# Sample columns of a state-space stage: joined on chip, or stored within the prompt's rows

## The chip, the cores and the metric

The kernel runs on one core of one Trainium2 chip. Its time is the device time of one launch in microseconds (us); lower is better. Three runs of the kernel before took 3122.86, 3125.23 and 3131.07 us; the median is 3125.23 us.

## The reference

One inference step of one decoder layer, in float32, for a prompt of 2048 tokens and for 8 samples of 4 tokens each, with the same weights. The part that the change touches is the S5 group: 512 of the channels of `h @ w_in` form 32 groups of 16, and each group drives a complex diagonal state of 64 entries.

```python
h = rms_norm(x, p['norm_mix'])
z = h @ p['w_in']
u, xin, bg, cg = jnp.split(z, ...)
y_ssm, s_re, s_im = s5_ssm(u, ...)          # s[t] = a * s[t-1] + B u[t];  y = Re(C s) + D u
y_ssm = jax.nn.gelu(y_ssm)
y_ssm = y_ssm * jax.nn.sigmoid(y_ssm @ p['w_glu'] + p['b_glu'])
conv_y, conv_buf = causal_dwconv(cg * xin, p['conv_w'], conv_prev)
y_conv = bg * conv_y
mixed = jnp.concatenate([rms_norm(y_ssm, ...), rms_norm(y_conv, ...)], axis=-1)
x = x + mixed @ p['w_out']
```

The prompt starts from a zero state, the samples from given states. The last states of both (`s_re`, `s_im`) are outputs. Cross-attention and a ConvFFN follow; the change leaves them alone.

## The kernel before

The tokens are cut into five pieces of 416 columns (`NP`); the fifth holds 384 columns of the prompt and the 32 of the samples. Every float32 weight and input is split into a high and a low part, and a product is three matmuls (`mm3`, L367 to L369). The program is one order written out by hand: TensorE (PE) works through the large products, and after each group of matmuls a hook lets the small streams (Python generators) issue a step. A `yield PAUSE` in a stream means "go on at the next hook". Every engine executes its own instructions strictly in the order in which they were issued.

**First stage** (to about 197 us): `u = h @ w_in`, piece by piece. `u_out` (L781) multiplies each tile of `u` by the row norm on GpSimd (POOL, L786) and stores it: the prompt's columns into `u_d`, of 256 columns for each of 8 token offsets, and the samples' 32 columns into a DRAM tensor of their own, `us_d`.

**Conv stage** (about 185 to 672 us): PE computes the short-conv group, 20 conv tiles (four channel tiles by five pieces), each of eight groups of nine matmuls on `mm` banks with a hook behind each: 160 hooks in all. After each conv tile follow `conv_in`, `conv_mid` and `conv_out` on VectorE (DVE), ScalarE (ACT) and POOL. The state-space work rides on the hooks as a stream called `slow`, made of three generators one after another:

- `state_inputs` (L951): 16 rounds of two groups. A round loads `uc` (128 partitions, two groups of 264 columns) from `u_d` (`load_u`, L861), multiplies by `gc` on PE (L994), and copies the result into `st` on ACT (L996, L997). DVE and POOL turn and scan `st` meanwhile. A round takes two or three hooks.
- `scan` (L1142): combines the blocks of the scan, and puts out the samples' last states (`sf`, L1147) by two transposes on PE (L1137).
- `state_outputs` (L1047): 16 rounds of four hooks. `back` (L1062) prepares a block on DVE (L1065, L1067, L1068) and POOL (L1069); `enter` (L1072) builds `scat`, what PE multiplies with, on DVE and POOL (L1081), with the samples' starting states copied in (L1075), and takes the prompt's last state from the block's last column (`sfin`, L1084). PE then makes two pairs of products (L1115 with `uc`, L1116 with `scat`) with a hook between them, and ACT applies GELU (L1117). Round c's `uc` and `scat` have two buffers each.

The samples come into these rounds by copies on POOL. All 32 groups of them are loaded from `us_d` once (L966), and in each round eight columns per group are joined to the tile that the DMA has filled:

```python
G.tensor_copy(out=uc[:, :, 256:264], in_=us_[:, 0, 2 * c:2 * c + 2, :])     # L989, state_inputs
G.tensor_copy(out=uc[:, :, 256:264], in_=us_[:, 1, 2 * c:2 * c + 2, :])     # L1108, state_outputs
G.tensor_copy(out=ysm[:, g2, :], in_=yg[:, :, 256:264])                     # L1123, the way out
```

The results go to `y_d`, the samples' through `ysm` to `ys_d`, and `p3_load` (L1325 on) reads both at the start of the next stage, the fifth piece first.

All DMAs named here go through one queue, SyncE's (SP), in order: the weights (`wraw`, L86), the inputs of the conv stage (`araw`, L176), the loads of the rounds, and the stores (L258), which are collected and issued at the next tick.

Of the kernel before, what the change touches and what calls it, by code (L numbers as in the profile page):

```python
# [208 lines left out]
def tile_hymba_step(ctx: ExitStack, tc: tile.TileContext, I: dict, O: list):  # L209
# [22 lines left out]

    x0_d, x1_d, x2_d = per_piece("x0"), per_piece("x1"), per_piece("x2")
    h3_d, o_d, yc_d = per_piece("h3"), per_piece("oo"), per_piece("yc", 4)
    u_d = dt("u_d", [512, NB, NCH])
    us_d = dt("us_d", [512, NT, 8])
    y_d = dt("y_d", [512, NB, NCH])
    ys_d = dt("ys_d", [512, NT, 8])
    kd_d = dt("kd_d", [256, 512])
    to_d = dt("to_d", [128, 32, 2, 128])  # L240
    g_d = dt("g_d", [128, 32, 128])
# [539 lines left out]
    def u_out(p, us):  # L781
        yield PAUSE
        w, c0 = CW[p], CPP * p
        for j in range(4):
            u = us[j]
            G.tensor_tensor(out=u, in0=u, in1=rs_p[p], op=ALU.mult)  # L786
            store(out=u_d[j * 128:(j + 1) * 128, :, c0:c0 + w], in_=u[:, 0:8 * w].rearrange("p (s c) -> p s c", s=8))
            if p == 4:
                store(out=us_d[j * 128:(j + 1) * 128], in_=u[:, 384:416].rearrange("p (s c) -> p s c", s=NT))
            yield  # L790

    rate[0] = 2
    srate[0] = 1
    slow.add(load_params())
# [64 lines left out]
    us_ = sp_.tile([128, 2, 32, 8], F32, name="us")  # L859

    def load_u(c):  # L861

        uc = py.tile([128, 2, 264], F32, tag="uc", name="uc", bufs=2)
        for i in range(2):
            g = 2 * c + i
            SY.dma_start(out=uc[:, i, 0:NCH], in_=u_d[16 * g:16 * g + 16].rearrange("p s c -> s p c"))
        return uc


# [81 lines left out]
    def state_inputs():  # L951
        ld = {}

        def load(c):
            g2 = slice(2 * c, 2 * c + 2)
            uc = load_u(c)
            gc = py.tile([128, 2, 2, 128], F32, tag="tcn", name="gc", bufs=2)[:, :, 0, :]
            SY.dma_start(out=gc, in_=g_d[:, g2, :])
            ld[c] = (uc, gc)

        G.memset(us_, 0.0)
        tb = phases()
        load(0)
        usv = us_d.rearrange("(g p) j b -> j p g b", p=16)
        for j in range(NT):
            SY.dma_start(out=us_[16 * j:16 * j + 16, 1], in_=usv[j])  # L966
        load(1)
        for _ in range(4):
            yield PAUSE
        V.tensor_copy(out=us_[64:128, 0], in_=us_[0:64, 1])  # L970
        ready, turned, scanned = False, 0, 0

        def recur(upto, n):

# [12 lines left out]
        for c in range(16):
            uc, gc = ld.pop(c)
            G.tensor_copy(out=uc[:, :, 256:264], in_=us_[:, 0, 2 * c:2 * c + 2, :])  # L989
            recur(c, 1)  # L990
            yield PAUSE
            for i in range(2):
                ps = aux()
                PE.matmul(ps[:, 0:264], lhsT=gc[:, i, :], rhs=uc[:, i, :], start=True, stop=True)  # L994
                h = slice(i * 64, (i + 1) * 64)
                S.copy(out=st[h, 0, c, :], in_=ps[0:64, 0:264])  # L996
                S.copy(out=st[h, 1, c, :], in_=ps[64:128, 0:264])  # L997
# [48 lines left out]

    def state_outputs():  # L1047
        yd = y_d.rearrange("(g q) t c -> g t q c", q=16)
        ysd = ys_d.rearrange("(g q) j b -> j q g b", q=16)
        ysm = py.tile([128, 32, 8], F32, name="ysm")  # L1050
        ld = {}

        def load(c):
# [18 lines left out]
        def enter(c):  # L1072

            sc = py.tile([128, 2, 264], F32, tag="scat", name="scat", bufs=2)
            G.tensor_copy(out=sc[:, :, 256:264], in_=s0s[:, 2 * c:2 * c + 2, :])  # L1075
            V.memset(sc[:, :, 0:1], 0.0)
            m1, m2 = parts.pop(c)
            for a in range(2):
                h = slice(a * 64, (a + 1) * 64)
                for r in range(2):  # L1080
                    (G if r else V).tensor_tensor(out=sc[r * 64:(r + 1) * 64, a, 1:256], in0=m1[h, r, 0:255],  # L1081
                                                  in1=m2[h, r, 0:255], op=ALU.add if r else ALU.subtract)
            for r in range(2):
                G.tensor_tensor(out=sfin[:, r, c:c + 1], in0=m1[:, r, 255:256], in1=m2[:, r, 255:256],  # L1084
                                op=ALU.add if r else ALU.subtract)
            ent_[c] = sc

        ent_ = {}
# [13 lines left out]
        for c in range(16):  # L1102
            if c + 1 < 16:
                enter(c + 1)
            if c + 2 < 16:
                back(c + 2)
            uc, tcn, oc = ld.pop(c)
            G.tensor_copy(out=uc[:, :, 256:264], in_=us_[:, 1, 2 * c:2 * c + 2, :])  # L1108
            yield PAUSE
            sc = ent_.pop(c)  # L1110
            g2 = slice(2 * c, 2 * c + 2)
            yg = py.tile([128, 2, 264], F32, tag="yg", name="yg", bufs=2)
            for i in range(2):
                ps = aux()
                PE.matmul(ps[:, 0:264], lhsT=tcn[:, i, :], rhs=uc[:, i, :], start=True, stop=False)  # L1115
                PE.matmul(ps[:, 0:264], lhsT=oc[:, i, :], rhs=sc[:, i, :], start=False, stop=True)  # L1116
                S.activation(out=yg[:, i, :], in_=ps[:, 0:264], func=AF.Gelu_apprx_tanh)  # L1117
                if i == 0:
                    yield PAUSE
            if c + 2 < 16:  # L1120
                load(c + 2)
            yield PAUSE
            G.tensor_copy(out=ysm[:, g2, :], in_=yg[:, :, 256:264])  # L1123
            for i in range(2):
                store(out=yd[2 * c + i], in_=yg[:, i, 0:256])
            yield PAUSE
        for j in range(NT):
# [5 lines left out]
    def state_out(pl, src, n, dsts):  # L1133

        for i in range(2):
# [3 lines left out]
            V.tensor_copy(out=e[0:n], in_=ps[0:n, 0:128])  # L1139
            store(out=dsts[i], in_=e[0:n])  # L1140

    def scan():  # L1142
# [991 lines left out]
```

## Time and profile before

| what | value |
|---|---|
| median of three runs | 3125.23 us |
| the profiled execution, its own time | 3123.47 us |
| its span, first to last instruction | 3121.3 us |
| PE busy | 2899.6 us (93%) |
| DVE busy | 1461.2 us (47%) |
| ACT busy | 1109.9 us (36%) |
| POOL busy | 1180.9 us (38%) |
| mean granted clock of TensorE | 0.969 of full speed |

"Busy" is the time that an engine spent on instructions; what matters here is the rest: time in which PE stands idle, and the instruction that ended that idle time. The clock column (PEclk) is the TensorE clock granted over a stretch, as a share of full speed: 1.0 is 2.4 GHz, and the engine's other level, 1.2 GHz, is 0.5. A stretch with a value between them had both.

### The profile page before, as it was taken

The page shows a single profiled execution, that of the slowest core. Times are in us where ns is not written, and L with a number is a line of the kernel's source. Part 1 is how long each engine was busy: PE and PEld are TensorE (multiplying, and loading weights), DVE is VectorE, ACT ScalarE, POOL GpSimd, SP SyncE. Part 2 cuts the span into 40 slices and gives each one's busy share as a digit, 9 for nine tenths or more (in the row PEclk, how much of TensorE's full clock was granted, in tenths as well). Part 3 has the DMA queues.
Part 4 walks back from the last instruction along what each step waited for, and adds up shares of the span by engine and source line. Part 5 has one row for each costly group of instructions (what it writes and reads, how often), then busy time and mean ns, then how long its engine had stood idle before and what let it go on. Part 6 is the DMA issues. An engine that isn't in the chain of part 4 may idle for free.

```text
span 3121.3 us, 41741 instructions
## 1 busy us (share of the span) xinstructions
PE 2899.6 (93%) x15536; PEld 2794.6 (90%) x15536; DVE 1461.2 (47%) x2698; ACT 1109.9 (36%) x2152; POOL 1180.9 (38%) x1352
## 2 busy tenths in 40 slices
PE   8867857798999999999999999999999999999998
PEld 7767856687999999999999999999999999999997
DVE  5747844445444434345453334345433333355544
ACT  5334322145444444433332232224322222243332
POOL 3654464435334001335343322324223323245554
PEclk9888978899999999999999999999999999999999
DMA  8454432237335112555642121213312112134331
GB/s 231 135 151 119 115 119 89 87 111 219 110 106 162 62 56 66 166 189 197 212 153 61 55 61 54 61 55 117 122 56 61 57 59 62 48 108 138 108 112 55
DMA packets 387337, 335.91 MB, mean 108 GB/s; under 512 B 81121, under 2 KB 361239, under 8 KB 387103
## 3 DMA queue, kind: packets, MB, share of 16 engines
q1 hardware_dynamic: 364079, 299.30, 32.2%
q10 hardware_dynamic: 23056, 33.96, 3.0%
q8 instruction: 122, 2.00, 0.3%
q14 instruction: 80, 0.66, 0.1%
HBM read 259.98 MB, written 75.29 MB: 107 GB/s over the span
## 4 chain that ended last, share of the span: by engine, by line
PE 55%; DVE 2%; DMA 2%; issue 1%; POOL 1%; ACT 1%; SPq 0%; ACTq 0%; DVEq 0%; POOLq 0%
PE g L368 5%; PE g L369 5%; PE g L367 5%; PE u L368 5%; PE d L367 5%; PE u L367 5%; PE u L369 5%; PE d L369 5%; PE d L368 5%; PE mm L368 3%; PE mm L367 3%; PE mm L369 3%; DMA out_dram<-orow 1%; PE aux L368 1%; POOL wlo L98 1%
## 5 line engine op out<-in xcount | busy, mean ns | idle before, releaser
L98 POOL TENSOR_TENSOR wlo<-wraw,whi 128x512 fp32r<-128x512 f32 x489 | 644.0, 1340 | 895.7 <-ACT whi L94 846.9
L367 PE MATMUL mm<-xh,whi 128*128 128x416 f32 x1600 | 596.9, 373 | 3.6 <-ACT whi L94 3.1
L368 PE MATMUL mm<-xl,whi 128*128 128x416 f32 x1600 | 575.2, 360 | 4.5 <-POOL xl L159 4.5
L369 PE MATMUL mm<-xh,wlo 128*128 128x416 f32 x1600 | 572.2, 358 | 3.0 <-POOL wlo L98 2.8
L2023 DVE TENSOR_TENSOR xac<-d,xac 128x416 f32<-128x416 f32 x440 | 258.2, 590 | 252.6 <-PE d L369 250.2
L367 PE MATMUL d<-acth,whi 128*128 128x416 f32 x880 | 311.3, 354 | 18.1 <-DVE xac L2023 16.9
L94 ACT CAST whi<-wraw 128x1024 fp32r<-128x1024 f32 x256 | 266.9, 1045 | 172.0 <-PE d L368 129.8
L367 PEld LDWEIGHTS mm<-xh,whi 128*128 128x128 f32 x1600 | 311.6, 195 | 14.2 <-ACT whi L94 3.8
L368 PEld LDWEIGHTS mm<-xl,whi 128*128 128x128 f32 x1600 | 311.1, 194 | 10.8 <-POOL xl L159 5.9
L369 PEld LDWEIGHTS mm<-xh,wlo 128*128 128x128 f32 x1600 | 310.1, 194 | 7.8 <-POOL wlo L98 4.9
L368 PE MATMUL u<-xl,whi 128*128 128x416 f32 x880 | 312.0, 355 | 1.4 <-POOL xl L159 0.7
L368 PE MATMUL g<-xl,whi 128*128 128x416 f32 x880 | 311.9, 354 | 0.0
L367 PE MATMUL g<-xh,whi 128*128 128x416 f32 x880 | 310.6, 353 | 0.0
L367 PE MATMUL u<-xh,whi 128*128 128x416 f32 x880 | 309.8, 352 | 0.8 <-ACT xh L158 0.6
L369 PE MATMUL g<-xh,wlo 128*128 128x416 f32 x880 | 309.7, 352 | 0.0
L369 PE MATMUL d<-acth,wlo 128*128 128x416 f32 x880 | 309.6, 352 | 0.0
L369 PE MATMUL u<-xh,wlo 128*128 128x416 f32 x880 | 308.5, 351 | 0.0
L368 PE MATMUL d<-actl,whi 128*128 128x416 f32 x880 | 308.0, 350 | 0.2 <-DVE actl L2004 0.2
L1183 DVE SCALAR_TENSOR_TENSOR t<-E,par,t 128x416 f32<-128x416 f32 (+1 forms) x220 | 153.9, 700 | 266.8 <-ACT t L1991 264.2
L159 POOL TENSOR_TENSOR xl<-araw,xh 128x416 fp32r<-128x416 f32 x100 | 115.1, 1153 | 418.0 <-ACT xh L158 386.5
L367 PEld LDWEIGHTS d<-acth,whi 128*128 128x128 f32 x880 | 165.2, 188 | 27.3 <-DVE xac L2023 24.6
L2000 DVE TENSOR_TENSOR t<-t,g 128x416 f32<-128x416 f32 x110 | 64.4, 586 | 260.4 <-PE g L369 260.3
(463 smaller groups left out, 4947.2 us busy)
## 6 DMA issues: line engine op xcount, KB each, us to landing
wraw<-in_w_up_dram SPq DMA_DIRECT2D x66, 512.0 KB
wraw<-in_w_gate_dram SPq DMA_DIRECT2D x66, 512.0 KB
wraw<-in_w_down_dram SPq DMA_DIRECT2D x66, 512.0 KB
araw<-x SPq DMA_DIRECT2D x120, 208.0 KB
xres<-x SPq DMA_DIRECT2D x80, 208.0 KB
x<-xo ACTq DMA_DIRECT2D x80, 208.0 KB
x<-xT ACTq DMA_DIRECT2D x40, 208.0 KB
araw<-oo SPq DMA_DIRECT2D x40, 208.0 KB
```

The source lines that it names most:

```text
L94: self.nc.scalar.copy(out=hi, in_=r)
L98: eng.tensor_tensor(out=lo[:, s], in0=r[:, s], in1=hi[:, s], op=ALU.subtract)
L159: (eng or nc.vector).tensor_tensor(out=lo[:, 0:n], in0=src, in1=hi[:, 0:n], op=ALU.subtract)
L367: PE.matmul(ps, lhsT=wh, rhs=xh, start=start, stop=False)
L368: PE.matmul(ps, lhsT=wh, rhs=xl, start=False, stop=False)
L369: PE.matmul(ps, lhsT=wl, rhs=xh, start=False, stop=stop)
L1183: V.scalar_tensor_tensor(out=out[:, 0:n], in0=E[:, tap * w:tap * w + n], scalar=c, in1=out[:, 0:n], op0=ALU.mult, op1=ALU.add)
L2000: V.tensor_tensor(out=t, in0=t, in1=ps_[:, 0:NP], op=ALU.mult)
L2023: V.tensor_tensor(out=x, in0=ps[:, 0:NP], in1=x, op=ALU.add)
```

## The change

`u_d` gets 272 columns for each token offset and `y_d` 264, so that the samples' columns stand behind the prompt's 256 in the same rows. For the fifth piece `u_out` multiplies into one of two tiles `ends` (zeroed once) by three POOL operations: the prompt's 48 columns, the samples in columns 256 to 264 at token offsets 0 to 3 (what L1108 joined), and the samples again in columns 264 to 272 at offsets 4 to 7 (what L989 joined). One store writes it all. The loads of the rounds bring the joined tile; the copies L989, L1108 and L1123, the tile `us_` with its loads, memset and copy, and `us_d` and `ys_d` go. The products of `state_inputs` have 272 columns, `st` too. The copy of the starting states in `enter` moves from POOL to ACT. The 32 one-column operations on `sfin` become six on DVE at the end of `scan`. The samples' last states are put out at the end of `state_outputs`, and the pauses around the two removed steps go: a round of `state_outputs` now takes three hooks. `p3_load` reads the samples from `y_d`.

```diff
-    u_d = dt("u_d", [512, NB, NCH])
-    us_d = dt("us_d", [512, NT, 8])
-    y_d = dt("y_d", [512, NB, NCH])
-    ys_d = dt("ys_d", [512, NT, 8])
+    u_d = dt("u_d", [512, NB, 272])
+    y_d = dt("y_d", [512, NB, 264])
...
     def u_out(p, us):
...
-            G.tensor_tensor(out=u, in0=u, in1=rs_p[p], op=ALU.mult)
-            store(out=u_d[j * 128:(j + 1) * 128, :, c0:c0 + w], in_=u[:, 0:8 * w].rearrange("p (s c) -> p s c", s=8))
-            if p == 4:
-                store(out=us_d[j * 128:(j + 1) * 128], in_=u[:, 384:416].rearrange("p (s c) -> p s c", s=NT))
+            cols = slice(j * 128, (j + 1) * 128)
+            if p < 4:
+                G.tensor_tensor(out=u, in0=u, in1=rs_p[p], op=ALU.mult)
+                store(out=u_d[cols, :, c0:c0 + w], in_=u[:, 0:8 * w].rearrange("p (s c) -> p s c", s=8))
+            else:
+                e = ends[j % 2]
+                for o, a, n in ((e[:, :, 0:w], 0, 8), (e[:, 0:NT, w:w + 8], 384, NT), (e[:, NT:8, w + 8:w + 16], 384, NT)):
+                    z = slice(a, a + n * (w if a == 0 else 8))
+                    G.tensor_tensor(out=o, in0=u[:, z].rearrange("p (s c) -> p s c", s=n),
+                                    in1=rs_p[p][:, z].rearrange("p (s c) -> p s c", s=n), op=ALU.mult)
+                store(out=u_d[cols, :, c0:c0 + w + 16], in_=e)
...
     def state_inputs():
...
-        G.memset(us_, 0.0)
...
-        for j in range(NT):
-            SY.dma_start(out=us_[16 * j:16 * j + 16, 1], in_=usv[j])
...
-        V.tensor_copy(out=us_[64:128, 0], in_=us_[0:64, 1])
...
-            G.tensor_copy(out=uc[:, :, 256:264], in_=us_[:, 0, 2 * c:2 * c + 2, :])
...
     def state_outputs():
...
-            G.tensor_copy(out=sc[:, :, 256:264], in_=s0s[:, 2 * c:2 * c + 2, :])
+            S.copy(out=sc[:, :, 256:264], in_=s0s[:, 2 * c:2 * c + 2, :])
...
-            for r in range(2):
-                G.tensor_tensor(out=sfin[:, r, c:c + 1], in0=m1[:, r, 255:256], in1=m2[:, r, 255:256],
-                                op=ALU.add if r else ALU.subtract)
...
-            G.tensor_copy(out=uc[:, :, 256:264], in_=us_[:, 1, 2 * c:2 * c + 2, :])
             yield PAUSE
...
             yield PAUSE
-            G.tensor_copy(out=ysm[:, g2, :], in_=yg[:, :, 256:264])
             for i in range(2):
-                store(out=yd[2 * c + i], in_=yg[:, i, 0:256])
-            yield PAUSE
-        for j in range(NT):
-            store(out=ysd[j], in_=ysm[j * 16:(j + 1) * 16])
+                store(out=yd[2 * c + i], in_=yg[:, i, :])
+        yield PAUSE
+        state_out(sp_, sf_.pop().rearrange("p r b g -> p r (b g)"), 128,
...
     def scan():
...
-        yield PAUSE
-        yield PAUSE
-        yield PAUSE
-        state_out(sp_, sf.rearrange("p r b g -> p r (b g)"), 128,
...
+        V.tensor_tensor(out=t, in0=ek[:, :, :, 15], in1=rp[:, :, 15].unsqueeze(1).to_broadcast(SE), op=ALU.mult)
+        V.tensor_tensor(out=t, in0=t, in1=last[:, :, :, 15], op=ALU.add)
...
     def p3_load(p):
...
-                SY.dma_start(out=y[:, 384:416].rearrange("p (s c) -> p s c", s=NT), in_=ys_d[j * 128:(j + 1) * 128])
+                SY.dma_start(out=y[:, 384:416].rearrange("p (s c) -> p s c", s=NT), in_=y_d[j * 128:(j + 1) * 128, 0:NT, 256:264])
```

POOL's order in the middle of `state_outputs`, one conv tile of the kernel before (`scat` is the right side of L1116, `st` the block, `ysm` the samples' results, `y` the conv tile):

```order
L1201 COPY halc<-E 128x2
L1271 TENSOR_TENSOR y<-y,rs_133 128x416
L1123 COPY ysm<-yg 128x16
L159 TENSOR_TENSOR xl<-araw,xh 128x416
L1075 COPY scat<-s0s 128x2x8
L1081 TENSOR_TENSOR scat<-st,mb 64x255 x2
L1084 TENSOR_TENSOR sfin<-st,mb 128x1 x2
L1069 TENSOR_TENSOR st<-st,ph 128x2x256
L1108 COPY uc<-us 128x2x8
```

and the like place with the change:

```order
L1202 COPY halc<-E 128x2
L1272 TENSOR_TENSOR y<-y,rs_131 128x416
L1079 TENSOR_TENSOR scat<-st,mb 64x255 x2
L1067 TENSOR_TENSOR st<-st,ph 128x2x256
L159 TENSOR_TENSOR xl<-araw,xh 128x416 x2
```

Of a round only `scat` and `st` are left on POOL; nothing that PE needs for the product with `uc` is issued there any more.

POOL's order at the end of the first stage, where the fifth piece of `u` goes out and the conv stage's inputs (`xl`) and weights (`wlo`) follow, in the kernel before:

```order
L786 TENSOR_TENSOR u<-u,rs_137 128x416 x4
L159 TENSOR_TENSOR xl<-araw,xh 128x416 x3
L98 TENSOR_TENSOR wlo<-wraw,whi 128x512 x2
L961 MEMSET us 128x512
L98 TENSOR_TENSOR wlo<-wraw,whi 128x512 x2
L159 TENSOR_TENSOR xl<-araw,xh 128x416
L98 TENSOR_TENSOR wlo<-wraw,whi 128x512 x4
L989 COPY uc<-us 128x2x8
```

and with the change:

```order
L792 TENSOR_TENSOR ends_169<-u,rs_135 128x8x48
L792 TENSOR_TENSOR ends_169<-u,rs_135 128x4x8 x2
L792 TENSOR_TENSOR ends_170<-u,rs_135 128x8x48
L792 TENSOR_TENSOR ends_170<-u,rs_135 128x4x8 x2
L792 TENSOR_TENSOR ends_169<-u,rs_135 128x8x48
L792 TENSOR_TENSOR ends_169<-u,rs_135 128x4x8 x2
L792 TENSOR_TENSOR ends_170<-u,rs_135 128x8x48
L792 TENSOR_TENSOR ends_170<-u,rs_135 128x4x8 x2
L159 TENSOR_TENSOR xl<-araw,xh 128x416 x3
L98 TENSOR_TENSOR wlo<-wraw,whi 128x512 x4
L159 TENSOR_TENSOR xl<-araw,xh 128x416
L98 TENSOR_TENSOR wlo<-wraw,whi 128x512 x4
```

Twelve operations into two tiles in turn stand where four stood, ahead of the same `xl`; the first join, behind eight `wlo`, is gone.

SP's order where the rounds of `state_inputs` begin (`gc` is the matrix of L994), before:

```order
L866 DMA uc<-u_d 128x1x256 x2
L958 DMA gc<-g_d 128x2x128
L966 DMA us<-us_d 16x32x8 x4
L866 DMA uc<-u_d 128x1x256 x2
L958 DMA gc<-g_d 128x2x128
```

and with the change:

```order
L872 DMA uc<-u_d 128x1x272 x2
L964 DMA gc<-g_d 128x2x128
L872 DMA uc<-u_d 128x1x272 x2
L964 DMA gc<-g_d 128x2x128
```

The four loads of the samples' columns, of 512 pieces of 32 bytes each, no longer stand between the loads of the first two rounds.

## Rows read from the trace of the kernel before

**Rows 1.** The page's part 2, the span in 40 slices, PE.

```profile
PE   8867857798999999999999999999999999999998
```

**Rows 2.** Busy time by stretch: PE, PEld, DVE, ACT, POOL, then PEclk, DMA share, GB/s.

```profile
215.00:335.00 120.00, 97.00 (x460) 89.41 (x461) 89.57 (x158) 54.10 (x126) 55.55 (x62) 0.92 0.42 122
...
388.00:625.00 237.00, 162.54 (x687) 147.52 (x686) 105.10 (x155) 49.70 (x102) 116.22 (x166) 0.83 0.32 97
632.00:672.00 40.00, 38.58 (x206) 37.04 (x205) 12.34 (x29) 10.67 (x23) 15.48 (x20) 1.00 0.29 85
```

**Rows 3.** Waits of PE, 190 to 640 us: total, times, longest.

```profile
PE aux L1115 <- POOL uc L1108: 74.5, 15, 11.9
PE aux L994 <- POOL uc L989: 23.0, 9, 10.1
PE aux L994 <- POOL dz L903: 17.1, 1, 17.1
PE aux L1137 <- DVE sf L1147: 8.5, 1, 8.5
```

**Rows 4.** Timeline of PE, 384 to 454 us: start, duration, instruction, idle before.

```profile
385.27 0.35 PE L367 MATMUL mm<-xh,whi 128*128 128x416 f32 x1
...
385.84 0.35 PE L367 MATMUL mm<-xh,whi 128*128 128x416 f32 x1
...
400.70 1.25 PE L1115 MATMUL aux<-uc,tcn 128*128 128x264 f32 x2 [11.87 <-POOL uc L1108]
...
452.91 0.61 PE L1115 MATMUL aux<-uc,tcn 128*128 128x264 f32 x2
...
453.60 0.55 PE L367 MATMUL mm<-xh,whi 128*128 128x416 f32 x1
```

**Rows 5.** Timeline of POOL, 388 to 401 us.

```profile
389.16 6.18 POOL L98 TENSOR_TENSOR wlo<-wraw,whi 128x512 fp32r<-128x512 f32 x4
...
397.39 1.49 POOL L1081 TENSOR_TENSOR scat<-st,mb 64x255 f32<-64x255 f32 x2
398.96 0.33 POOL L1084 TENSOR_TENSOR sfin<-st,mb 128x1 f32<-128x1 f32 x2
399.25 1.25 POOL L1069 TENSOR_TENSOR st<-st,ph 128x512 f32<-128x512 f32 x1
400.45 0.19 POOL L1108 COPY uc<-us 128x16 f32<-128x16 f32 x1
```

**Rows 6.** Timeline of DVE, 388 to 520 us.

```profile
392.59 1.63 DVE L1067 TENSOR_TENSOR st<-st,mc 128x512 f32<-128x512 f32 x1
...
444.68 0.41 DVE L1081 TENSOR_TENSOR scat<-st,mb 64x255 f32<-64x255 f32 x1 [9.49 <-issue]
...
445.58 0.70 DVE L1065 TENSOR_TENSOR mc<-ek,rp 128x512 f32<-128x512 f32 x1
...
447.46 1.12 DVE L1068 TENSOR_TENSOR mb<-st,ph 128x512 f32<-128x512 f32 x1
...
510.88 0.59 DVE L1251 TENSOR_TENSOR xi<-mm,rs 128x416 f32<-128x416 f32 x1 [3.39 <-PE mm L369]
...
515.48 0.59 DVE L1270 TENSOR_TENSOR y<-y,mm 128x416 f32<-128x416 f32 x1
```

**Rows 7.** Timelines of POOL, SP and DVE, 182 to 216 us.

```profile
186.23 4.96 POOL L786 TENSOR_TENSOR u<-u,rs 128x416 f32<-128x416 f32 x4 [1.24 <-ACT rs L438]
...
199.81 1.37 SPq L866 DMA_DIRECT2D uc<-u_d  x2
...
201.72 2.05 SPq L966 DMA_DIRECT2D us<-us_d  x4
...
206.34 0.70 DVE L970 COPY us<-us 64x256 f32<-64x256 f32 x1 [6.93 <-DMA uc<-u_d]
```

**Rows 8.** Waits of SP's DMA queue, 0 to 800 us.

```profile
SPq L258 <- POOL y L1271: 62.3, 11, 10.9
```

**Rows 9.** Groups of instructions of DVE by line, 388 to 625 us.

```profile
L162 DVE SCALAR_TENSOR_TENSOR xl<-araw,par,xh 128x416 fp32r<-128x416 f32 x16 | 13.0, 811 | 41.7 <-ACT xh L161 41.7
```

More of the change, by code (lines that the diff above doesn't have):

```diff
@@ L785, in u_out @@
             u = us[j]
-            G.tensor_tensor(out=u, in0=u, in1=rs_p[p], op=ALU.mult)
-            store(out=u_d[j * 128:(j + 1) * 128, :, c0:c0 + w], in_=u[:, 0:8 * w].rearrange("p (s c) -> p s c", s=8))
-            if p == 4:
-                store(out=us_d[j * 128:(j + 1) * 128], in_=u[:, 384:416].rearrange("p (s c) -> p s c", s=NT))
+            cols = slice(j * 128, (j + 1) * 128)
[9 more added lines that the diff above has]
+                store(out=u_d[cols, :, c0:c0 + w + 16], in_=e)
             yield
+    ends = [p1.tile([128, NB, 64], F32, name=f"ends{i}") for i in range(2)]
+    for e in ends:
+        G.memset(e, 0.0)
     rate[0] = 2
@@ L853, in tile_hymba_step @@
     sp_ = ss_.enter_context(pool("states", side="left"))
-    st = sp_.tile([128, 2, 16, 264], F32, name="st")
+    st = sp_.tile([128, 2, 16, 272], F32, name="st")
     s0 = sp_.tile([128, 2, 8, 16], F32, name="s0")
@@ L857, in tile_hymba_step @@
     py = spy.enter_context(pool("py", side="right"))
-    us_ = sp_.tile([128, 2, 32, 8], F32, name="us")
     def load_u(c):
-        uc = py.tile([128, 2, 264], F32, tag="uc", name="uc", bufs=2)
+        uc = py.tile([128, 2, 272], F32, tag="uc", name="uc", bufs=2)
         for i in range(2):
             g = 2 * c + i
-            SY.dma_start(out=uc[:, i, 0:NCH], in_=u_d[16 * g:16 * g + 16].rearrange("p s c -> s p c"))
+            SY.dma_start(out=uc[:, i, :], in_=u_d[16 * g:16 * g + 16].rearrange("p s c -> s p c"))
         return uc
@@ L959, in load @@
             ld[c] = (uc, gc)
-        G.memset(us_, 0.0)
         tb = phases()
         load(0)
-        usv = us_d.rearrange("(g p) j b -> j p g b", p=16)
-        for j in range(NT):
-            SY.dma_start(out=us_[16 * j:16 * j + 16, 1], in_=usv[j])
         load(1)
@@ L993, in state_inputs @@
                 ps = aux()
-                PE.matmul(ps[:, 0:264], lhsT=gc[:, i, :], rhs=uc[:, i, :], start=True, stop=True)
+                PE.matmul(ps[:, 0:272], lhsT=gc[:, i, :], rhs=uc[:, i, :], start=True, stop=True)
                 h = slice(i * 64, (i + 1) * 64)
-                S.copy(out=st[h, 0, c, :], in_=ps[0:64, 0:264])
-                S.copy(out=st[h, 1, c, :], in_=ps[64:128, 0:264])
+                S.copy(out=st[h, 0, c, :], in_=ps[0:64, 0:272])
+                S.copy(out=st[h, 1, c, :], in_=ps[64:128, 0:272])
             if c + 2 < 16:
@@ L1048, in state_outputs @@
         yd = y_d.rearrange("(g q) t c -> g t q c", q=16)
-        ysd = ys_d.rearrange("(g q) j b -> j q g b", q=16)
-        ysm = py.tile([128, 32, 8], F32, name="ysm")
         ld = {}
@@ L1107, in state_outputs @@
             uc, tcn, oc = ld.pop(c)
-            G.tensor_copy(out=uc[:, :, 256:264], in_=us_[:, 1, 2 * c:2 * c + 2, :])
             yield PAUSE
             sc = ent_.pop(c)
-            g2 = slice(2 * c, 2 * c + 2)
             yg = py.tile([128, 2, 264], F32, tag="yg", name="yg", bufs=2)
@@ L1114, in state_outputs @@
                 ps = aux()
-                PE.matmul(ps[:, 0:264], lhsT=tcn[:, i, :], rhs=uc[:, i, :], start=True, stop=False)
+                PE.matmul(ps[:, 0:264], lhsT=tcn[:, i, :], rhs=uc[:, i, 0:264], start=True, stop=False)
                 PE.matmul(ps[:, 0:264], lhsT=oc[:, i, :], rhs=sc[:, i, :], start=False, stop=True)
@@ L1122, in state_outputs @@
             yield PAUSE
-            G.tensor_copy(out=ysm[:, g2, :], in_=yg[:, :, 256:264])
             for i in range(2):
-                store(out=yd[2 * c + i], in_=yg[:, i, 0:256])
-            yield PAUSE
-        for j in range(NT):
-            store(out=ysd[j], in_=ysm[j * 16:(j + 1) * 16])
+                store(out=yd[2 * c + i], in_=yg[:, i, :])
+        yield PAUSE
+        state_out(sp_, sf_.pop().rearrange("p r b g -> p r (b g)"), 128,
+                  [o[0].rearrange("b (g a) n -> (b g) (a n)", a=2) for o in (sre_s, sim_s)])
+        yield PAUSE
         state_out(sp_, sfin, 16, [o[0, 0].rearrange("(g a) n -> g (a n)", a=2) for o in (sre_p, sim_p)])
@@ L1140, in state_out @@
             store(out=dsts[i], in_=e[0:n])
+    sf_ = []
     def scan():
@@ L1146, in scan @@
         cmul(sp_, sf[:, 0], sf[:, 1], s0[:, 0], s0[:, 1], a4[:, 0:1, :].to_broadcast(sh), a4[:, 1:2, :].to_broadcast(sh), sh, "scm")
-        V.tensor_tensor(out=sf, in0=sf, in1=st[:, :, :, 256:264].rearrange("p r g b -> p r b g"), op=ALU.add)
-        yield PAUSE
-        yield PAUSE
-        yield PAUSE
-        state_out(sp_, sf.rearrange("p r b g -> p r (b g)"), 128,
-                  [o[0].rearrange("b (g a) n -> (b g) (a n)", a=2) for o in (sre_s, sim_s)])
+        V.tensor_tensor(out=sf, in0=sf, in1=st[:, :, :, 264:272].rearrange("p r g b -> p r b g"), op=ALU.add)
+        sf_.append(sf)
         yield
@@ L1174, in scan @@
         V.memset(ek[:, :, :, 0:1], 0.0)
+        yield
+        SE = [128, 2, 16]
+        t, m2 = (sp_.tile(SE, F32, tag="sfe", name="sfe", bufs=2) for _ in range(2))
+        V.tensor_tensor(out=t, in0=ek[:, :, :, 15], in1=rp[:, :, 15].unsqueeze(1).to_broadcast(SE), op=ALU.mult)
+        V.tensor_tensor(out=t, in0=t, in1=last[:, :, :, 15], op=ALU.add)
+        V.tensor_tensor(out=m2, in0=t[:, ::-1], in1=ph[:, 1, :, 15].unsqueeze(1).to_broadcast(SE), op=ALU.mult)
+        V.tensor_tensor(out=t, in0=t, in1=ph[:, 0, :, 15].unsqueeze(1).to_broadcast(SE), op=ALU.mult)
+        for r, op in ((0, ALU.subtract), (1, ALU.add)):
+            V.tensor_tensor(out=sfin[:, r], in0=t[:, r], in1=m2[:, r], op=op)
         yield
```

## Prediction

> **What bounds the kernel now.** I read the page's slices first. From slice 11 to 39 PE is busy in at least nine tenths of every slice; only the small step 5 below reaches that far [rows 1]. What can be won lies ahead of that, in the conv stage, so I read busy time by stretch next. From 632 to 672 us, where no round of the state-space work is left, PE is busy 38.6 of 40 us at the full clock (PEclk 1.00, that is 2.4 GHz). From 388 to 625 us, the 16 rounds of `state_outputs`, it is busy 162.5 of 237 us at 0.83, a mixture of 2.4 and 1.2 GHz [rows 2]. The other engines have room there: DVE 105, ACT 50, POOL 116 of 237 us.
>
> The waits of PE say who ends the idle time: 74.5 us until the join of `uc` in `state_outputs` (L1108), 23.0 us until the join in `state_inputs` (L989), once 17.1 us at the first of these rounds, and 8.5 us for the samples' last states (L1137 on `sf`) [rows 3]. The 17.1 us are put down to a memset of `dz` that was issued right behind the first join; the first product needs the join, not the memset.
>
> The timeline shows why a copy of 0.19 us holds PE for 11.9 us [rows 4, 5]. POOL works in order: four splits of weights (6.2 us), two halves of `scat` for the next round (1.5), `sfin`, `st` for the round after (1.25), and only then the copy on which PE waits. The queue ahead of the copy is the cost, not the copy.
>
> **The price of PE's work.** Three matmuls take 0.57 us at full clock, so a hook (nine) takes 1.71 us; a pair of products of L1115 and L1116 takes 0.69 us [rows 4]. The 16 rounds hold 16 x 4 - 3 = 61 hooks and 32 pairs: 61 x 1.71 + 22.1 = 126.4 us. The stretch took 237 us; 74.5 are waits, and the remaining 36 are matmuls at the low clock, which I read as following the stalls.
>
> **The change, part by part.**
>
> 1. *Rounds of `state_outputs`.* With L1108 gone, L1115 needs only loads issued two rounds ahead, and L1116 needs a `scat` that was issued a round ahead. Two pauses become one, so a round has three hooks: 16 x 3 - 2 = 46 hooks and 32 pairs, 100.8 us for PE alone; the 15 hooks set free run behind without rounds, 25.7 us. What is late next is the chain through DVE and POOL. In one round `enter` and `back` hold DVE from 444.68 to 448.58, 3.90 us [rows 6], then `st` on POOL takes 1.25 [rows 5] before the next `enter`: 5.15 us, 82.4 for 16. Each conv tile holds DVE from 510.88 to 516.07, 5.19 us with its wait for ACT [rows 6]; 46 hooks hold 5.75 tiles, 29.8 us. Splitting inputs (`xl`) takes 13.0 us over 61 hooks [rows 9], 9.8 over 46. The four weight splits ahead of the second `scat` add 6.2 [rows 5]. Sum 128.2, more than PE's 100.8, so I take it: 128.2 + 25.7 = 153.9 against 237, **-83 us**. Ends: PE alone gives 126.5 (-110); if half the waits and half the low-clock loss stay, 126.5 + 55 (-55).
>
>    Do DVE and POOL get in each other's way? A DVE operation on 512 elements takes 0.70 us alone and 1.63 beside a weight split [rows 6]; the splits take 1.55 each in that run, and a POOL operation of that size 1.25 alone [rows 5]. So a pair takes 1.63, not 0.70 + 1.25 = 1.95: they hinder each other, but overlap in part. My 3.90 us already holds that hindrance (1.12 us for one of the three). The Trainium skill, page "SBUF — State Buffer", section "Who interferes with whom", is stricter: a VectorE operation with two inputs in SBUF and a GpSimd operation that reads SBUF fully block each other for the whole instruction. By that rule the total would be 3038 us (worked out under the rivals); the 1.63 agrees with it only in part.
>
> 2. *Rounds of `state_inputs`, 215 to 335 us.* Some 44 hooks and 32 single products (half a pair, 0.35 us): 86.4 us of 120. The rest is the 23.0 us of waits and 10.6 of low clock. The join goes, but DVE is busy 89.6 of the 120 us [rows 2], and ACT, which empties the banks of L994 in order, stands behind copies that wait for DVE's scans. I let about half of the waits come back there: 23 + 3 of clock - 12 = **-14 us**; ends 0 and -34.
>
> 3. *The first product (17.1 us).* Without the join it waits for its loads. These now start later: POOL's four operations on `u` took 4.96 us, 1.24 each [rows 7]; each tile gets two small ones more (0.19 as the copy in [rows 5]), and the third tile waits until the first store has landed, about 2.6 us after its issue (the load of the samples ends its issue at 203.77, DVE starts on it at 206.34) [rows 7]. POOL is then free 2.9 us later, and SP, which stands behind the `xl` on POOL, issues the first `uc` at 202.7 instead of 199.8. Two loads of 1.4 us, 0.5 for `gc` (estimated like one of the four in 2.05 us) and 2.6 to land: 207.2 instead of 214.9. **-7 us**; ends +3 (only the delay stays) and -12.
>
> 4. *The samples' last states.* The transposes move to the end of `state_outputs`, where `sf` is long ready: **-8.5 us**; ends 0 (another wait in the same place, since DVE's scan chain there is kept) and -12 with the clock. The six operations that replace `sfin` add 1 to 2 us to DVE ahead of round 0, inside the same slack.
>
> 5. *`p3_load`.* Four loads of 128 pieces become four of 512 pieces of 32 bytes at the start of the next stage. Four such loads were issued in 2.05 us and landed 2.6 us later [rows 7]. **+3 us**; ends 0 and +6.
>
> 6. *Nothing for the rest.* The 64 small POOL operations that go cost PE only through the waits counted above. The 16 copies now on ACT meet an engine that is busy 50 of 237 us [rows 2]; should it be late, L1116 waits. Eight columns more in 32 products are 0.3 us. The two memsets stand at the start, ahead of loads that POOL awaits anyway; if uncovered, about 1 us.
>
> Sum: -83 - 14 - 7 - 8.5 + 3 = -109.5. The profiled execution took 3123.5 us, 1.8 below the median; 3014 for it, **3016 us** for the median.
>
> **The rivals.**
>
> *DVE and POOL strictly in turn.* If each of the three operations of `back` had to wait out a POOL operation (0.70 + 0.75) they would take 4.35 us instead of 3.0: 16 x 1.35 = +22, **3038 us**. For it: 1.63 beside a split. Against it: the pair's 1.95.
>
> *SP's queue takes the place of the join.* At a conv tile's end SP stands up to 10.9 us for POOL's `y` [rows 8], and the loads of a later round stand behind. They need 10.9 + 1.4 + 2.6 = 14.9 us; from the end of a round's products to the use of what is loaded then there are five hooks and two pairs, 9.9. Six tiles x 5.0 = 30, with the low clock (36 per 74.5) 44: **3060 us**. Against it: in the trace these 10.9 us hold PE's own stall, which shrinks.
>
> *PE alone.* No chain is late: -27 in part 1 and -20 in part 2, **2969 us**.
>
> *The wait only changes its name.* PE waits as long for `scat`, which POOL also makes; only parts 3 to 5 remain: 3111 us. Against it: the products with `scat` follow those with `uc` without idle time [rows 4].
>
> *Slower: the longer rows.* A row of `u_d` now has 1088 bytes instead of 1024. If such loads land late, all 32 rounds wait. The point that decides is 9.9 us from issue; they take about 4 now. To lose all of the gain and 9.4 us more, each must take 13.6; at 14 us the loss is 32 x 4.1 = 131, **3147 us**. Nothing in the trace hints at a factor of three.
>
> **How the numbers follow.** Forecast 0.64, strict turns 0.15, SP's queue 0.09, PE alone 0.04, wait renamed 0.05, longer rows 0.03. A measurement of this kernel tells 0.3%, or 9.4 us, from no change. Renamed waits end at 3111, just beyond that; I give 0.03 of them to "same" and 0.02 to "faster". So faster 0.94, same 0.03, slower 0.03. The range takes in SP's queue with the upper ends of parts 2, 4 and 5 beside it in part, and most of the way to the lower ends (all of them at once give 2957): 2978 to 3078 us.
>
> **What would show it.** Right: no wait on `uc`; PEclk above 0.92 in the rounds of `state_outputs`, which take about 130 us; PE's remaining waits ended by `scat` of DVE or POOL, a few us at each conv tile; the first product at about 207 us. Wrong: PE idle more than 40 us in these rounds, whoever ends it; loads of `uc` as releasers; or the stage's gain given back where the next one starts.

## The result, and the profile after

| | before | after | ratio after/before (95% interval) |
|---|---|---|---|
| median of the runs, us | 3125.2 (3122.9 to 3131.1) | 3035.6 (3033.1 to 3038.7) | 0.9711 (0.9694 to 0.9728) |
| span of the profiled execution, us | 3121.3 | 3034.5 | |
| mean granted clock of TensorE, share of full speed | 0.969 | 0.979 | |

The change is faster by 2.9%. I had forecast 3016 us, a gain of 109 us; it is 90. The direction and the place were right; a fifth of the gain did not come.

Marks read from the two traces split the 86.8 us of span into five stretches. A mark is the start of the first or last instruction of a group; where PE stands waiting in front of the output rounds, in before, it is the start of the last matmul ahead of the wait. A gain is negative:

| stretch | before | after | difference | forecast |
|---|---|---|---|---|
| start to the first product L994 | 214.9 | 207.4 | -7.6 | -7 |
| first to last product L994 (`state_inputs`) | 108.3 | 104.9 | -3.4 | -14 |
| from there until PE reaches the output rounds | 65.3 | 60.8 | -4.5 | -8.5 |
| output rounds and the hooks behind them, to the first load of `yr` | 282.8 | 208.9 | -73.9 | -83 |
| first load of `yr` to the end | 2450.0 | 2452.5 | +2.5 | +3 |

The slices of the page of after, against [rows 1], counted from 1: slices 11 and on look as before, and slices 6 to 8, which stood at 5, 7 and 7 tenths, stand at 7, 9 and 9.

```profile
PE   8878979989999999999999999999999999999998
```

Busy time by stretch, after (columns as in [rows 2]): the rounds of `state_inputs`, the output rounds, and two stretches behind them.

```profile
207.00:313.00 106.00, 88.97 (x401) 82.14 (x402) 89.56 (x176) 49.56 (x115) 48.70 (x47) 0.90 0.51 140
373.00:509.00 136.00, 114.40 (x545) 105.69 (x544) 108.17 (x152) 46.60 (x106) 89.51 (x86) 0.92 0.52 158
509.00:536.00 27.00, 27.00 (x146) 26.53 (x146) 9.60 (x19) 8.27 (x16) 7.58 (x8) 1.00 0.33 95
536.00:582.00 46.00, 44.58 (x237) 42.95 (x236) 15.43 (x34) 13.25 (x28) 17.09 (x21) 1.00 0.24 76
```

The output rounds took 237 us before and take 136 now, at a granted clock of 0.92 in place of 0.83. The 27 us behind them hold the freed hooks: PE is never idle there, at 2.4 GHz. DVE, which was busy for 105 of 237 us, is busy for 108 of 136: the same work in a little over half the time.

The waits of PE, after, 190 to 560 us (columns as in [rows 3]):

```profile
PE aux L994 <- DMA gc<-g_d: 19.5, 5, 5.7
PE aux L1108 <- DMA tcn<-to_d: 14.0, 6, 4.7
PE aux L1109 <- POOL scat L1079: 4.1, 1, 4.1
PE mm L366 <- POOL xl L159: 3.9, 1, 3.9
PE aux L1108 <- DVE mc L1063: 3.6, 1, 3.6
PE aux L514 <- ACT st L997: 2.8, 1, 2.8
```

In the output rounds 74.5 us of waits for the join became 14.0 + 4.1 + 3.6 = 21.7 us. Of the 19.5 us for the loads of `gc`, 5.7 are the wait of the first product, where 17.1 us had been. So in the rounds of `state_inputs` 23.0 us for the join became 13.8 us for `gc` and 2.8 us for `st` (L514), 16.6 in all: there the wait was mostly renamed. Why loads are late is in SP's timeline (start, duration, instruction) and in the waits of SP's queue over the output rounds, both of after:

```profile
380.35 0.33 SPq L256 DMA_DIRECT2D yc<-y  x1
...
383.17 0.38 SPq L86 DMA_DIRECT2D wraw<-in_w_in_dram  x1
...
395.68 1.22 SPq L872 DMA_DIRECT2D uc<-u_d  x2
397.00 0.40 SPq L1055 DMA_DIRECT2D tcn<-to_d  x1
```

```profile
SPq L256 <- POOL y L1272: 30.5, 6, 9.0
SPq L176 <- POOL xl L159: 20.0, 9, 4.3
SPq L86 <- POOL wlo L98: 12.6, 5, 4.6
```

Round 0 ends on PE at about 377 us, but the loads that it frees buffers for are issued at 395.68, behind stores and other loads that wait for POOL (20.7 us of such waits between 376.5 and 396.5 us). PE needs that `tcn` in round 2 and waits 4.7 us for it, by its timeline:

```profile
402.11 1.22 PE L1108 MATMUL aux<-uc,tcn 128*128 128x264 f32 x2 [4.71 <-DMA tcn<-to_d]
```

Apart from 4.1 us at `scat`, POOL's order no longer holds PE directly in these rounds; it does so, more weakly, through SP's.

### The profile page after: what moved, and what is told of

Same layout as the page of the kernel before. It is cut to its first block, busy times and chain, and to the rows that moved or that the text cites. A ratio compares the mean times of both kernels' runs of the same rounds, so it can differ in the third digit from the quotient of the medians.

```text
span 3034.5 us, 41684 instructions
## 1 busy us (share of the span) xinstructions
PE 2885.5 (95%) x15536; PEld 2787.0 (92%) x15536; DVE 1473.8 (49%) x2703; ACT 1111.9 (37%) x2168; POOL 1154.7 (38%) x1265
## 4 chain that ended last, share of the span: by engine, by line
PE 55%; DVE 3%; DMA 2%; ACT 1%; issue 1%; POOL 1%; SPq 0%; ACTq 0%; DVEq 0%; POOLq 0%
PE g L366 5%; PE d L365 5%; PE g L367 5%; PE g L365 5%; PE u L366 5%; PE d L367 5%; PE d L366 5%; PE u L365 5%; PE u L367 5%; PE mm L366 3%; PE mm L365 3%; PE mm L367 3%; DMA out_dram<-orow 1%; DVE t L1184 1%; PE aux L366 1%
```

## The experiments

No experiment leaves out any of the computation. Each was timed in 3 rounds (the last four in 5) beside the kernel before on the same chip; ratios are to that kernel, with 95% intervals.

### Which part of the change brings the gain

**b_join_act**: before, with nothing changed but the engine of the two joins.

```
-G.tensor_copy(out=uc[:, :, 256:264], in_=us_[:, 0, 2 * c:2 * c + 2, :])
+S.copy(out=uc[:, :, 256:264], in_=us_[:, 0, 2 * c:2 * c + 2, :])
```
(and the same at L1108, with `us_[:, 1, ...]`)

> The kernel before with both joins (L989 and L1108) moved from POOL to ACT, all other operations, tensors and pauses as before. Theory: the join leaves the queue of scat, sfin and st and ACT has room (50 of 237 us busy), so most of the gain comes without any change in DRAM: 3045 to 3080 us. Rival (the gain comes from the number of operations that POOL loses, or from the joined rows in DRAM): 3110 us or more.

Measured: 3030.6 us, ratio 0.9693 (0.9675 to 0.9711): the whole gain, beyond what I expected. PE's waits in it, 190 to 560 us:

```profile
PE aux L994 <- ACT uc L989: 18.1, 4, 14.8
PE aux L994 <- DMA gc<-g_d: 13.5, 3, 5.6
PE aux L1115 <- ACT uc L1108: 9.8, 4, 3.8
PE aux L1137 <- DVE sf L1147: 9.3, 1, 9.3
```

The same copy, in the queue of an engine that is not behind, holds the output rounds for 9.8 us in place of 74.5. No column was joined in DRAM, no hook taken away, no POOL operation removed but the joins. Of the 18.1 us at L989, 14.8 are the first product's. The `gc` waits of after stand here too, 13.5 us against 13.8 in the same rounds, so they do not come from the longer rows.

**b_join_act_out**: the same edit at L1108 alone.

> The kernel before with only the join of state_outputs (L1108) moved to ACT; the join of state_inputs (L989) stays on POOL. Theory (PE pays for POOL's queue ahead of a join, and in the rounds of state_inputs DVE's turning and scanning would hold PE even without it): nearly all of the gain of moving both, 3035 to 3050 us. Rival (each join costs what the waits on it add up to): the 23.0 us and 17.1 us of L989 stay, 3060 us or more.

Measured: 3040.4 us, 0.9721 (0.97 to 0.9743). The output rounds carry most of it; the other join, still on POOL, holds PE for 22.8 us, as before.

**b_short_queue**: before, with POOL's other small operations taken away (`sfin` as the six DVE operations of the change; `s0s` and `ysm` copied on ACT) and both joins left on POOL.

```
-G.tensor_copy(out=sc[:, :, 256:264], in_=s0s[:, 2 * c:2 * c + 2, :])
+S.copy(out=sc[:, :, 256:264], in_=s0s[:, 2 * c:2 * c + 2, :])
-G.tensor_copy(out=ysm[:, g2, :], in_=yg[:, :, 256:264])
+S.copy(out=ysm[:, g2, :], in_=yg[:, :, 256:264])
```

> The kernel before with POOL's other small operations taken away (sfin by the six operations on DVE, the starting states and ysm copied on ACT), but with both joins left on POOL. Theory (the join costs because it stands in order behind scat, st, the conv tile's y and the splits, which stay): a small part of the gain, 3090 to 3115 us. Rival (POOL had too many operations, and the join was only the last of them): 3060 us or less.

Measured: 3121.4 us, 0.9979 (0.9968 to 0.9991): almost nothing, less than either theory gave. POOL's timeline at one join (start, duration, instruction, idle before and its releaser) and the wait of PE from 190 to 640 us:

```profile
447.43 0.82 POOL L1081 TENSOR_TENSOR scat<-st,mb 64x255 f32<-64x255 f32 x1
450.39 1.28 POOL L1069 TENSOR_TENSOR st<-st,ph 128x512 f32<-128x512 f32 x1 [2.15 <-DVE mb L1068]
451.62 0.20 POOL L1105 COPY uc<-us 128x16 f32<-128x16 f32 x1
```

```profile
PE aux L1112 <- POOL uc L1105: 69.3, 15, 11.6
```

POOL was busy for 18 us less in these rounds (98.1 us, against 116.2 in [rows 2]), and PE waited 5 us less. POOL is idle for 2.15 us ahead of this join: it is not short of time, it stands at `st`, which needs a product of DVE. Such waits were 1.2 us in before; here they are, by POOL's waits from 393 to 623 us,

```profile
POOL st L1069 <- DVE mb L1068: 15.0, 8, 2.1
```

I had read the queue ahead of the join as POOL's own work. At about half of the joins it is a chain through both engines; at others, the first among them, the splits of weights stand ahead as in [rows 5], and they stayed. Of what was tried here, only leaving the queue helped.

**b_three_hooks**: before without the pause behind the stores of `yg` (one line `yield PAUSE` removed), so three hooks per round as in after.

> The kernel before with the pause behind the stores removed and nothing else, so that a round of state_outputs takes three hooks with all joins on POOL. Theory: PE meets the join behind the same queue of POOL and waits longer per round for what it saves in hooks: 3110 to 3130 us. Rival (the gain comes from shorter rounds): 3075 us or less.

Measured: 3122.6 us, 0.999 (0.9981 to 0.9999), and 67.4 us of waits for the join. Shorter rounds alone bring next to nothing.

### Where the missing 20 us went

**a_four_hooks**: after, with that pause put back.

> The changed kernel with a pause put back behind the stores, so that a round of state_outputs takes four hooks again. Theory (what PE waited for was POOL's queue ahead of the join, and what is left are loads that come late behind SP's queue): the 15 hooks only move from behind the rounds into them, each load gets 1.7 us more, and of the 21.7 us that PE still waits in these rounds some go: 3025 to 3040 us. Rival (the gain comes from shorter rounds): most of the 74 us of these rounds is given back, 3085 us or more.

Measured: 3030.2 us, 0.9693 (0.9677 to 0.9709), not told apart from after. The hook costs nothing here.

**a_sf_early**: after, with the samples' last states put out in `scan` again, after three pauses.

> The changed kernel with the samples' last states put out in scan again, with its three pauses, as before. Theory (the transposes make PE wait there for DVE's chain): PE waits for sf again, 6 to 9 us, 3040 to 3045 us. Rival (DVE's chain is on the path either way, PE waits for it a little later): 3034 to 3038 us.

Measured: 3034.4 us, 0.9698 (0.9683 to 0.9714), not told apart from after. PE waits for `sf` again, 10.9 us, so it reaches the output rounds 9.3 us later (382.4, not 373.1 us), but starts their last product only 2.2 us later. PE's wait there is not on the path; I take it that the chain of DVE behind it needs that time anyhow.

**a_loads_act**: after, with the loads of `uc`, `gc` and `tcn` issued on ACT's queue.

```
-SY.dma_start(out=gc, in_=g_d[:, g2, :])
+S.dma_start(out=gc, in_=g_d[:, g2, :])
```

> The changed kernel with the loads of the rounds (uc, gc, tcn) issued on ACT's queue instead of SP's. Theory (these loads come late because they stand on SP behind stores that wait for POOL and behind weights and inputs that wait for buffers): the 33.5 us that PE waits for gc and tcn fall by half or more, with some of the low clock: 3000 to 3025 us. Rival (the transfers themselves take that long, or ACT's own waits hold the loads as SP's did): 3033 us or more.

Measured: 3034.3 us, 0.9709 (0.9694 to 0.9723): the theory missed. PE's waits, 190 to 560 us:

```profile
PE aux L994 <- ACT st L997: 11.3, 4, 5.3
PE aux L1109 <- POOL scat L1079: 8.9, 3, 4.5
PE aux L994 <- DMA gc<-g_d: 6.5, 2, 4.6
PE aux L514 <- ACT st L997: 5.3, 1, 5.3
PE aux L1108 <- ACT yg L1110: 5.0, 3, 3.3
```

The waits for loads shrink from 33.5 us to about 7.5 (1.0 us for `tcn` is not among these rows), and about as much comes up under other names.

**a_turn_pool**: after, with every second block of `state_inputs` turned on POOL (in after: every third).

```
-turn(turned, G if turned % 3 == 1 else V)
+turn(turned, G if turned % 2 == 1 else V)
```

> The changed kernel with every second turn of a block on POOL instead of every third (8 of 16 instead of 5), 6 to 7 us less for DVE in the rounds of state_inputs. Theory (these rounds are held by DVE, busy 90 of 106 us): they get 4 to 8 us shorter, 3026 to 3033 us. Rival (they are held by the loads, of which gc ends 19.5 us of PE's waits): no change, 3033 to 3038 us, and PE waits for gc as long.

Measured: 3044.4 us, 0.973 (0.9711 to 0.9748): no gain. The median lies 9 us above that of after and above both forecasts; the intervals do not tell the two kernels apart. Groups of DVE's instructions (line, tile, shapes, count, busy us, mean ns, idle before) in the rounds of `state_inputs`, of after and then of this kernel:

```profile
L955 DVE TENSOR_TENSOR_SCAN st<-dz,st 128x256 f32<-128x256 f32 x28 | 27.9, 1035 | 8.2 <-ACT dz L952 4.4 <-POOL st L948 3.8
L162 DVE SCALAR_TENSOR_TENSOR xl<-araw,par,xh 128x416 fp32r<-128x416 f32 x9 | 7.8, 864 | 1.3 <-ACT xh L161 1.3
```

```profile
L955 DVE TENSOR_TENSOR_SCAN st<-dz,st 128x256 f32<-128x256 f32 x26 | 29.1, 1160 | 8.8 <-ACT dz L952 4.9 <-POOL st L948 3.9
L162 DVE SCALAR_TENSOR_TENSOR xl<-araw,par,xh 128x416 fp32r<-128x416 f32 x9 | 9.2, 1025 | 1.3 <-ACT xh L161 1.3
```

Two of the turns left DVE within this stretch, but what stayed there became longer: a scan 1160 ns in place of 1035, an `xl` 1025 in place of 864.

**a_two_dz** and **al_two_dz**: after, and `a_loads_act`, with two tiles for the scan's multipliers.

```
-S.copy(out=dz[:, :, 1:16], in_=rp[:, c, 0:1].unsqueeze(1).to_broadcast([128, 16, 15]))
+z = dzs[c % 2]
+S.copy(out=z[:, :, 1:16], in_=rp[:, c, 0:1].unsqueeze(1).to_broadcast([128, 16, 15]))
```

> The changed kernel with two tiles for the scan's multipliers (dz) in place of one, so that ACT's copy for the next block need not wait for DVE's scan of the one before (14.3 us of ACT's waits in the first-product rounds). Theory (several chains of about one length hold these rounds; the longest for TensorE is the loads behind SP's queue, 19.5 us by gc): the dz waits leave ACT, gc's stay, 3032 to 3038 us. Rival (ACT's waits for the scans were the one thing that held the rounds, as the prediction's second term had it): gc's waits fall too, 3020 to 3027.

> Two dz tiles and, besides, the loads of uc, gc and tcn issued from ACT's queue: the two suspected holds of the first-product rounds taken away together. Theory (SP's queue and ACT's dz wait each hold the rounds when the other is gone): TensorE's waits there fall from about 20 us to under 10, 3015 to 3028 us. Rival (DVE, busy 89.6 of 106 us, sets the pace of the rounds whatever the queues do): the waits move to the scat, st or xl names again, 3031 to 3037.

Measured: 3039.7 us, 0.9709 (0.9695 to 0.9722), just above the bounds of its theory, and 3036.1 us, 0.9703 (0.969 to 0.9717), within those of its rival. ACT's 14.3 us of waits for the scans fall to 0.2 us in the first kernel and 1.5 in the second, and PE waits about as long as before: 21.3 us for `gc` in the first, 14.2 and 7.0 for `st` in the second. The last rival holds best: in `state_inputs` neither queue sets the pace. DVE is busy 93.4 of 107 us in `al_two_dz`.

### Versions meant to beat both

**a_ys_apart**: after, with y's samples as before (gathered in `ysm`, by ACT; rows of 256; the fourth hook), `u` still joined in DRAM.

```
+S.copy(out=ysm[:, 2 * c:2 * c + 2, :], in_=yg[:, :, 256:264])
-store(out=yd[2 * c + i], in_=yg[:, i, :])
+store(out=yd[2 * c + i], in_=yg[:, i, 0:256])
+yield PAUSE
```

> The changed kernel with y's samples kept apart as before (rows of 256, gathered on chip by a copy that ACT makes instead of POOL, stored and loaded as their own), and the fourth hook per output round with them; u's joined rows and the shorter POOL queue stay. Theory (the longer y rows cost the last stage the 2 to 5 us seen from its first load to the end, and the fourth hook costs nothing): 3024 to 3031 us. Rival (the difference of the last stage isn't the rows'): 3030 to 3036.

Measured: 3027.6 us, 0.9674 (0.9661 to 0.9688). The number fits the theory, the reason does not: from the first load of `yr` to the end takes 2452.8 us here, with the old rows, and 2452.5 in after. Over all versions this stretch takes 2449.9 to 2455.6 us, in no order of the rows: 2449.9 in `a_sf_early` with the new rows, 2450.2 in `b_join_act` with the old. The samples' 32-byte pieces cost nothing that these marks show.

**c_best**: `al_two_dz` with the fourth hook.

> The changed kernel with two dz tiles, the loads on ACT's queue and four hooks per output round together. Theory (each frees one hold, they add): 3010 to 3025 us. Rival (DVE's pace and the clock set the rounds): 3028 to 3034, as with four hooks alone.

Measured: 3027.2 us (3020.8 to 3029.5), 0.9672 (0.9659 to 0.9685), just under the rival's bounds and above the theory's: the holds do not add. Against `al_two_dz` on the same chip (3033.1 to 3038.9) it differs by the hook alone and is about 9 us faster. The marks say how (us):

| | PE reaches the output rounds | start of the last product with `uc` (L1108 in after) | first load of `yr` |
|---|---|---|---|
| before | 388.5 | 623.6 | 671.3 |
| b_join_act | 388.5 | 533.4 | 581.2 |
| after | 373.1 | 508.2 | 582.0 |
| al_two_dz | 375.6 | 509.0 | 582.9 |
| c_best | 375.6 | 524.3 | 573.1 |

With four hooks the rounds take 15 us longer, and the 25 us of hooks that ran behind them are done inside: some 10 us of them cost nothing, in time in which PE would have waited (its idle time in the rounds falls from 19.6 to 12.7 us) or run at the lower clock. The versions with the fourth hook, `b_join_act` among them, reach ratios of 0.9672 to 0.9693 with overlapping intervals: two words changed in the kernel before are not told apart from the best that I found.

## Why the prediction was right, and where its sizes were not

*The bound and its cause.* Right, and shown: the queue ahead of the join is the cost (`b_join_act`). Joining in DRAM, fewer hooks and fewer POOL operations were not needed for the gain, and the last two alone bring next to nothing (`b_three_hooks`, `b_short_queue`). Of the signs set beforehand, no wait on `uc` and the first product at about 207 us came; the clock of the output rounds is 0.92, at the mark and not above it; they take 136 us, not 130; and their waits are ended by loads of `tcn` (14.0 of 21.7 us) more than by `scat` (4.1). With those loads on another queue `scat` holds PE for 8.9 us and the time is the same (`a_loads_act`), as it should be if the chain of DVE and POOL is the pace.

*Step 1, -83 us, measured -73.9.* I took the chain of DVE and POOL for what sets the 16 rounds, 128.2 us; they took 136. The freed hooks behind them took 26.1 us in place of 25.7 (from the last product to the first load of `yr` 72.8 us, against 46.7 before). DVE is idle for 27.8 us of the rounds, and only 4.5 of these are waits for PE, so PE seldom holds it up. The term that was mis-sized is the 5.15 us per round. The largest of DVE's groups by line in the output rounds of after (15 rounds of its work lie in the stretch):

```profile
L1079 DVE TENSOR_TENSOR scat<-st,mb 64x255 f32<-64x255 f32 x30 | 31.3, 1042 | 14.2 <-POOL st L1067 13.7
L1063 DVE TENSOR_TENSOR mc<-ek,rp 128x512 f32<-128x512 f32 x15 | 18.2, 1211 | 0.5
L1065 DVE TENSOR_TENSOR st<-st,mc 128x512 f32<-128x512 f32 x15 | 14.0, 931 | 0.5
L1066 DVE TENSOR_TENSOR mb<-st,ph 128x512 f32<-128x512 f32 x15 | 12.7, 848 | 0.5
L162 DVE SCALAR_TENSOR_TENSOR xl<-araw,par,xh 128x416 fp32r<-128x416 f32 x12 | 10.2, 862 | 0.4 <-ACT xh L161 0.4
L1184 DVE SCALAR_TENSOR_TENSOR y<-E,par,y 128x416 f32<-128x416 f32 (+1 forms) x14 | 9.2, 654 | 5.8 <-ACT y L1264 5.6
L1252 DVE TENSOR_TENSOR xi<-mm,rs 128x416 f32<-128x416 f32 x7 | 4.1, 585 | 3.2 <-PE mm L367 3.2
```

A round holds DVE for 2 x 1.04 + 1.21 + 0.93 + 0.85 = 5.07 us, and 13.7 / 15 = 0.91 us of waiting for POOL's `st` come on top: 5.98. The forecast had 5.15, or 5.54 with a round's share of the 6.2 us for weight splits that I had added apart. `scat` is the operation that I sized wrongly: in [rows 6] a half took 0.41 us, at a moment when POOL did next to nothing beside it (last section). The size stood in the trace of before, in the view of [rows 9]:

```profile
L1081 DVE TENSOR_TENSOR scat<-st,mb 64x255 f32<-64x255 f32 x30 | 24.2, 807 | 23.5 <-issue 23.0
L1067 DVE TENSOR_TENSOR st<-st,mc 128x512 f32<-128x512 f32 x14 | 18.0, 1286 | 0.5
L1068 DVE TENSOR_TENSOR mb<-st,ph 128x512 f32<-128x512 f32 x14 | 14.1, 1005 | 0.5
L1065 DVE TENSOR_TENSOR mc<-ek,rp 128x512 f32<-128x512 f32 x14 | 12.4, 889 | 0.4
```

By these means a round is 2 x 0.81 + 1.29 + 1.01 + 0.89 = 4.79 us of DVE and 1.25 of POOL, 6.04, close to the 5.98 that came.

A second term was off as well: operations of seven conv tiles fall into the stretch, not of 5.75, at about 5.2 us each as forecast. In sum, rounds with their idle time and `scat`'s memset took 94 us (forecast 88.6), conv tiles and `xl` 47 (39.6), and 5 us go off again because DVE's operations overlap a little (the groups add up to 113.3 us, the engine was busy for 108.2). So the sum missed by only 8 us in part by luck: it left out this overlap, and the overlap made up for some of what the two terms lacked.

The three operations of `back` take 2.99 us together, and I had 3.0. So the rival *DVE and POOL strictly in turn* (4.35 for those three, of which the 0.75 us of waiting for each stands on no row) fell; hindrance came where I had not looked. The sum also set the 15 freed hooks behind the rounds. That they could have run inside, in part in the chain's shadow, is what `c_best` shows against `al_two_dz`: the change gives about 9 us away by it.

*Step 2, -14, measured -3.4.* The step let half of the 23.0 us of waits come back, by ACT's copies, and 3 us of low clock go. 16.6 us came back, first by loads, and PE's busy time in the stretch rose by 3.0 us where it was to fall: 89.0 us at a clock of 0.90 in after (the first row of busy time above), against 86.0 at 0.91 in before,

```profile
215.00:324.00 109.00, 86.00 (x402) 78.52 (x403) 79.33 (x144) 48.19 (x115) 49.95 (x57) 0.91 0.40 118
```

Removing the loads' wait, ACT's wait for the scans, or both together gained nothing, and giving POOL more of DVE's work lengthened DVE's other operations. DVE is busy in 84% of the stretch in after and in 83 to 88% in its variants, so I take its work, stretched beside POOL's, for the pace. That is argued and not shown: no run of after lightened DVE without loading POOL, and in `b_join_act` DVE is busy for only 84.0 of 106.8 us (79%) and the stretch is no shorter. What sets the pace there stays open.

*Step 3, -7, measured -7.6.* The first product came at 207.4 us against 207.2, and by the steps foreseen. SP's timeline and PE's, of after:

```profile
202.32 1.36 SPq L872 DMA_DIRECT2D uc<-u_d  x2
203.73 0.46 SPq L964 DMA_DIRECT2D gc<-g_d  x1
```

```profile
207.36 2.15 PE L994 MATMUL aux<-uc,gc 128*128 128x272 f32 x4 [5.69 <-DMA gc<-g_d]
```

The first `uc` is issued at 202.32 (forecast 202.7), and from the end of the issue of `gc` to the product it takes 3.2 us where I had 2.6. That 2.6 was a loose reading: [rows 7] gives a load of `uc` as the releaser, not the load of the samples.

*Step 4, -8.5, measured -4.5 by the marks*: its worth for the total is nothing that a run can tell (`a_sf_early`), and I take it that DVE's chain, not the transpose, was on the path. *Step 5, +3, measured +2.5 by the marks*, but `a_ys_apart` has the same 2452.8 us without the small pieces, so the match is not this step's.

*The rivals.* SP's queue took the join's place in part: 14.0 us in the output rounds by `tcn`, against the 30 I had priced, and taking it away (`a_loads_act`) gave no time back. "The wait only changes its name" holds for `state_inputs`, 23.0 to 16.6 us, not for the output rounds. (Its 3111 us counts from the profiled execution; on the scale of the medians it would be 3113.)

## What to carry to other kernels

A tiny copy costs what stands ahead of it in its engine's order: ask of each small operation on which a busy engine waits what its queue holds, and what that in turn waits for, and move the copy before any data layout is changed. Waits summed under one name are not the gain from removing them; where the next chain is nearly as long, forecast from its sum, with operation times taken from places where the neighbour engine is as busy as it will be. When a chain on other engines sets the length of a loop, filler work belongs inside it, not behind.

## What I had not expected of the hardware

A DVE operation on 64 x 255 elements took 0.41 us at 444.68 us of before [rows 6]. POOL's timeline of before shows POOL idle until 445.12 us:

```profile
445.12 0.48 POOL L1123 COPY ysm<-yg 128x16 f32<-128x16 f32 x1 [4.11 <-ACT yg L1117]
```

In after two of them took 2.90 us, 1.45 each, while POOL ran splits of weights of 1.35 each. The two timelines of after, DVE and then POOL:

```profile
391.40 2.90 DVE L1079 TENSOR_TENSOR scat<-st,mb 64x255 f32<-64x255 f32 x2 [1.96 <-POOL st L1067]
```

```profile
391.32 2.69 POOL L98 TENSOR_TENSOR wlo<-wraw,whi 128x512 fp32r<-128x512 f32 x2
```

So a short operation grew by 1.04 us beside one of 1.35. In before, two halves of `scat` had taken 1.29 and 1.38 us (at 388.18 and 389.51 us), while POOL was busy with a product and with a split. Strictly in turn, with 1.25 us for a POOL operation alone [rows 5], the short operation and its neighbour would take 0.41 + 1.25 = 1.66 us, the larger one of the prediction 0.70 + 1.25 = 1.95; DVE's operations took 1.45 and 1.63. What I had not expected is that for the short one this is three and a half times its own length.

The Trainium skill, page "SBUF — State Buffer", section "Who interferes with whom", says that such a pair contend for a shared port under an exclusive lock, so that one waits out the other. The trace agrees with that rule in part, for the short operation (13% under strict turns) about as far as for the large one (16%).
